# Token mixer of a diffusion trunk: the level scores as column-tiled products of 32 keys

## The chip, the cores and the metric

The kernel runs on one core of a Trainium2 chip. Its time is the device time of one execution in microseconds. Times are given as the median of several executions; a profiled execution is one more, recorded by the hardware profiler, and its trace tells which instruction ran when.

## The reference

The program is a two-layer backbone over 256 latent tokens and 256 context tokens of width 1024. Each layer is a half-step SwiGLU feed-forward, a token mixer and a second half-step feed-forward, each behind a modulated RMSNorm. The mixer has one input projection, two groups of heads and one output projection. The change is in the second group, a bidirectional gated linear recurrence with four heads of width 128:

```python
def step(S, inp):                       # one chunk of 64 tokens, one direction
    qc, kc, gc, vc = inp
    b = jnp.cumsum(gc, axis=2)
    diff = b[:, :, :, None, :] - b[:, :, None, :, :]
    decay = jnp.exp(jnp.where(mask, diff, -jnp.inf))
    scores = jnp.einsum("bhtk,bhsk,bhtsk->bhts", qc, kc, decay)
    o = (jnp.einsum("bhts,bhsv->bhtv", scores, vc)
         + jnp.einsum("bhtk,bhkv->bhtv", qc * jnp.exp(b), S))
    ...
```

In words: the score of query t against key s is a sum over the 128 channels of query, key and the product of all forget gates between the two tokens; the forward direction uses keys at or before t, the backward direction keys at or after t, and the outputs of both are added. The latent tokens start from the context's final state. In layer 1 only that state is needed of the context, not its output.

## The kernel before, in words

All activations lie with channels on the partitions. Every large product (feed-forwards, input and output projection) is a sum of three TensorE products in a split format: weights and activations are kept as a high part (`whi`, `h_hi`, `g_hi`) and the remainder (`wlo`, `h_lo`, `g_lo`), written by `mm3` at lines 309, 310 and 311. A weight piece of 512 x 256 comes in by one DMA into one of three `wraw` buffers; ScalarE makes its high part (`split`, line 210), VectorE its low part (`low`, line 214), into one of four slots of 4,352 bytes per partition each (`slot`). `pump` (lines 158 to 185) issues these steps as buffers come free.

The program is emitted in one fixed order. `fm` calls `tick` after each set of products, and `tick` advances one or two generators ("lanes") that stand behind the projection: their steps are placed among the large products after a set amount of these. So each engine gets its instructions in a written-out order, and a `yield n` in a generator says how much projection work comes before its next step.

The recurrence is the generator `hgrn`, one per layer and pair of heads. It replaces the chunked scan by seven levels over 128-token chunks. At level `lev`, with b = 2^lev, `lev` is the highest bit in which the positions of a valid pair differ, so the two tokens lie in the two halves of one block of 2b tokens. `KB` (keys) and `QA` (queries) have been multiplied by the forget gates up to the block's middle, so a plain product over channels is the score. `keys` (line 536, ScalarE) builds `ka`, in which each key carries the decay of the direction that its half needs; `alternate` reads the matching queries from both directions' `QA` with an access pattern that changes buffer every b elements.

`scores` (line 549) makes, for each head of the pair and each 128-token chunk, one fp32 product of 128 keys by 128 queries: 8 products in layer 0 (four chunks), 4 in layer 1 (two chunks), per call. There are eight calls per pair: one for the diagonal (`ks`, copied into the score tile `ST` by ScalarE at line 559), one per level. TensorE carries out an fp32 product as two instructions, each with a weight load. A 128 x 128 result holds all pairs of a chunk, of which each level needs only some: VectorE's `copy_predicated` (line 581) puts those into `ST` under a byte mask, `masks`, 128 x 128 per level. Between the products and the `copy_predicated`, VectorE multiplies `KB` (line 569), `QA` (line 575) and the gates `F` (line 578) for the next level. The score products go into PSUM tiles from a pool of three, `aux`, which the gated MLP heads (`spatial`, line 790) and the normalisations share. One score call takes two of them in layer 0, one in layer 1.

After the levels, scores between the two chunks of a sequence go into the middle slots of `ST` (lines 587 to 591), and `ST` multiplies the values (line 629).

One other place in the kernel uses products with 32 columns of weights: `ada_rows` (line 281), which sums the modulation's partial results. It writes four products to the four groups of 32 PSUM partitions:

```python
for n, (lhs, rhs) in enumerate(parts):
    for c in range(4):
        nc.tensor.matmul(ps[32 * c:32 * c + 32, :], lhsT=lhs, rhs=rhs[:, P * c:P * c + P],
                         start=(n == 0), stop=(n == len(parts) - 1))
```

Of the kernel before, what the change touches and what calls it, by code (L numbers as in the profile page):

```python
# [12 lines left out]
U8 = mybir.dt.uint8  # L13
AF = mybir.ActivationFunctionType
# [3 lines left out]
P = 128  # L18
# [11 lines left out]
EPS = 1e-6  # L30
POS_THETA = 10000.0
NLEV = 7
LEAD = 64
GLEAD = 0

# [16 lines left out]


def level_masks():
    x = np.arange(P)[:, None] ^ np.arange(P)[None, :]
    m = np.stack([(x >> lev) == 1 for lev in range(NLEV)], axis=1)
    return np.ascontiguousarray(m.reshape(P, NLEV * P).astype(np.uint8))

# [14 lines left out]
class Trunk:  # L75
# [129 lines left out]
    def slot(self, part, lead):  # L205
        t = self.wp.tile([P, LEAD + 1024], F32R, tag=part, name="w" + part, bufs=self.N_SPLIT)
        return t[:, lead:lead + 1024].rearrange("p (k c) -> p k c", k=4)
# [99 lines left out]
    def mm3(self, ps, l_hi, l_lo, r_hi, r_lo, start, stop, swap=False):  # L307
        mm = self.nc.tensor.matmul
        mm(ps, lhsT=l_hi, rhs=r_hi, start=start, stop=False)  # L309
        mm(ps, lhsT=l_hi, rhs=r_lo, start=False, stop=False)  # L310
        mm(ps, lhsT=l_lo, rhs=r_hi, start=False, stop=stop)  # L311
# [207 lines left out]
    def hgrn(self, l, hp, mp, F, KB, q, V, ready, oT, ended):  # L519
        nc = self.nc  # L520
        last = l == DEPTH - 1
        nq = SEQ if last else T
        ns = nq // SEQ
        nb = nq // P
# [3 lines left out]
        QA = mp.tile([P, 2, 2, nq], F32, tag="QA", name="QA", bufs=two)  # L528
        ST = mp.tile([P, 2, ns, 4, P], F32, tag="ST", name="ST", bufs=two)
        tt = nc.vector.tensor_tensor  # L530

        def keys(lev):
            b = 1 << lev
            ka = mp.tile([P, 2, nq], F32, tag="ks", name="ka", bufs=2 * two)
            for d in range(2):
                nc.scalar.activation(self.halves(ka, b)[d], self.halves(KB[:, d, :, :nq], b)[d], AF.Copy)
            return ka

        def scores(lhs, rhs):

            r = []
            for h in range(2):
                if h == 0 or ns == 2:
                    sc = self.aux()
                    dst = ST[:, h, :, 0::3, :] if ns == 2 else ST[:, :, 0, 0::3, :]
                    r.append((dst, sc.rearrange("p (s c t) -> p s c t", c=2, t=P)))
                for c in range(nb):
                    o = (c + (0 if ns == 2 else nb * h)) * P
                    nc.tensor.matmul(sc[:, o:o + P], lhsT=lhs(h, c * P), rhs=rhs(h, c * P), start=True, stop=True)  # L549
            return r  # L550

        ks = mp.tile([P, 2, nq], F32, tag="ks", name="ks", bufs=2 * two)
        tt(ks, KB[:, 0, :, :nq], KB[:, 1, :, :nq], op=ALU.add)
        ka = keys(0)
        for d in range(2):
            tt(QA[:, 1 - d], q[:, :, :nq], F[:, d, :, :nq], op=mult)
        yield HP[l]
        for dst, sc in scores(lambda h, c: ks[:, h, c:c + P], lambda h, c: q[:, h, c:c + P]):
            nc.scalar.activation(dst, sc, AF.Copy)
        yield HQ[l]  # L560
        for lev in range(NLEV):
            b = 1 << lev
            sc = scores(lambda h, c: ka[:, h, c:c + P],
                        lambda h, c: self.alternate(QA[:, 0, h, c:c + P], QA[:, 1, h, c:c + P], b))
            n = T // b
            for d in range(2):
                t = F[:, d, :, :n].rearrange("p h (n two) -> p h n two", two=2)
                kh = self.halves(KB[:, d], b)[d]
                tt(kh, kh, t[:, :, :, 1 - d, None].to_broadcast([P, 2, n // 2, b]), op=mult)
            if lev < NLEV - 1:  # L570
                ka = keys(lev + 1)
            for d in range(2):
                tq = F[:, d, :, :nq // b].rearrange("p h (n two) -> p h n two", two=2)
                qh = self.halves(QA[:, 1 - d], b)[1 - d]
                tt(qh, qh, tq[:, :, :, d, None].to_broadcast([P, 2, nq // (2 * b), b]), op=mult)
            for d in range(2):
                t = F[:, d, :, :n].rearrange("p h (n two) -> p h n two", two=2)
                tt(F[:, d, :, :n // 2], t[:, :, :, 0], t[:, :, :, 1], op=mult)
            mk = self.masks[:, lev, None, None, :].to_broadcast([P, 2, 2, P])
            for dst, s_ in sc:  # L580
                nc.vector.copy_predicated(dst, mk, s_)
            yield pace
        for h in range(2):
            sc = self.aux()
            for s in range(ns):
                c0, c1 = slice(s * SEQ, s * SEQ + P), slice(s * SEQ + P, s * SEQ + SEQ)
                nc.tensor.matmul(sc[:, s * SEQ:s * SEQ + P], lhsT=KB[:, 0, h, c0], rhs=QA[:, 1, h, c1],
                                 start=True, stop=True)
                nc.tensor.matmul(sc[:, s * SEQ + P:s * SEQ + SEQ], lhsT=KB[:, 1, h, c1], rhs=QA[:, 0, h, c0],
                                 start=True, stop=True)  # L590
            nc.scalar.activation(ST[:, h, :, 1:3, :], sc[:, :nq].rearrange("p (s c t) -> p s c t", c=2, t=P), AF.Copy)
        for d in range(2):
            for h in range(2):
                a = P * (1 - d)
                x = QA[:, 1 - d, h, a:a + P]
                nc.vector.tensor_scalar(x, x, F[:, d, h, d:d + 1], None, op0=mult)
                a = SEQ + P * d
                x = KB[:, d, h, a:a + P]
# [15 lines left out]
        for h in range(2):  # L614
            head = slice((2 * hp + h) * P, (2 * hp + h + 1) * P)
            for d in range(2):
                o = ps[:, (2 * h + d) * P:(2 * h + d + 1) * P]
# [4 lines left out]
        for s in range(ns):  # L622
            ps = self.adp.tile([P, 512], F32, tag="ada", name="o")
            for c in range(2):
                for h in range(2):
                    head = slice((2 * hp + h) * P, (2 * hp + h + 1) * P)
                    o = ps[:, (2 * c + h) * P:(2 * c + h + 1) * P]
                    for e in range(2):
                        nc.tensor.matmul(o, lhsT=ST[:, h, s, 2 * e + c, :], rhs=V[:, 2 * s + e, head],  # L629
                                         start=(e == 0), stop=(e == 1 and s == 1))  # L630
                    if s == 0:
                        for d in range(2):
                            nc.tensor.matmul(o, lhsT=QA[:, 1 - d, h, c * P:(c + 1) * P], rhs=S[:, h, d, :],  # L633
                                             start=False, stop=(d == 1))
# [5 lines left out]
            r = self.rstd(ss[:, :4], 4, P)  # L640
# [227 lines left out]
    def start(self):  # L868
        nc = self.nc
        io = self.io  # L870
        cp = self.cp
# [16 lines left out]
        self.mods = cp.tile([P, DEPTH * N_MOD, 2, KT], F32, tag="mods", name="mods")  # L888
        self.lb = cp.tile([P, 2, 2, 4], F32, tag="lb", name="lb")
        self.vec = [cp.tile([P, P], F32, tag=f"vec{l}", name="vec") for l in range(DEPTH)]  # L890
        self.masks = cp.tile([P, NLEV, P], U8, tag="masks", name="masks")
        with self.tc.tile_pool(name="start", bufs=1) as st:
            self.table(AF.Silu)
            cc = st.tile([16, P], F32, tag="cc", name="cc")
# [4 lines left out]
            for l, names in enumerate((("norm_ffn1_g", "norm_mix_g", "norm_ffn2_g", "norm_final_g"),  # L899
# [4 lines left out]
                for nm in names:  # L904
                    r = io[nm]
                    if nm != "norm_final_g":
                        r = r.rearrange("l n -> (l n)")
                    r = r.rearrange("(k p) -> k p", p=P)
# [91 lines left out]
            r = self.token_rstd(LAT)  # L1000
# [105 lines left out]
```

## Time and profile before

| | |
|---|---|
| median of 3 executions | 1790.61 us (1787.4 to 1796.05) |
| profiled execution | 1787.99 us, its span 1786.2 us |
| layer 0 mixer, recurrence's levels | about 450 to 598 us of the span |
| layer 1 mixer, recurrence's levels | about 1449 to 1537 us |
| score products, TensorE busy | 44.7 us (levels) and 6.1 us (diagonal) |
| `copy_predicated`, VectorE busy | 29.2 us |

In the profile, PE is TensorE's products, PEld its weight loads, DVE VectorE, ACT ScalarE, SP the engine that issues the DMAs. A line such as `L549 PE MATMUL aux<-QA,ka 128*128 128x128 f32 x336 | 44.7, 285 | 0.0` reads: source line, engine, operation, output and inputs, weights (rows*columns), moving operand, number of instructions, then busy time in us, mean duration in ns, and idle time before. In a timeline, the first number is the start in us, the second the length of the merged run of instructions. Products overlap in TensorE's pipeline, so the distance between starts, not the duration, is the rate.

### The profile page before, as it was taken

What the parts mean: (1) busy time and instruction counts of PE and PEld (TensorE: products, weight loads), DVE (VectorE), ACT (ScalarE), POOL (GpSimd) and SP (SyncE); (2) the same over time, 40 slices, a digit from 0 to 9 for tenths busy, and PEclk for the clock granted to TensorE, in tenths of its full rate; (3) what the DMA queues carried; (4) which work ended last, traced back from release to release, by engine and by line L of the source; (5) the groups of instructions that cost most, each with busy time, mean ns of one, the idle gap of its engine ahead of it and who ended that gap; (6) DMA issues with size and microseconds to landing.
All of it is one profiled execution on the core that took longest, in us unless ns stands there. A gap on an engine that the chain in (4) does not pass through costs nothing. (4 is left out here: it accounts for less than half of the span.)

```text
span 1786.2 us, 27050 instructions
## 1 busy us (share of the span) xinstructions
PE 1753.0 (98%) x10853; PEld 1534.5 (86%) x10853; DVE 1129.6 (63%) x1746; ACT 670.5 (38%) x1087; POOL 19.6 (1%) x26
## 2 busy tenths in 40 slices
PE   6999999999999999999999999999999999989998
PEld 5788888899899898888888898888888999979998
DVE  4876676775737667666666676555545668665554
ACT  3422222236545344222222252223222565545543
POOL 0000000000000000000000000000000000000000
PEclk9999999999999999999999999999999999989999
DMA  8565655664212114555555545555454532446663
GB/s 315 166 177 162 178 160 165 180 188 139 71 60 83 60 60 144 151 157 160 151 153 158 178 137 157 161 154 159 156 167 153 160 107 83 130 125 195 194 186 128
DMA packets 230646, 266.65 MB, mean 149 GB/s; under 512 B 10369, under 2 KB 192377, under 8 KB 230521
## 3 DMA queue, kind: packets, MB, share of 16 engines
q1 hardware_dynamic: 230520, 264.93, 48.8%
q8 instruction: 85, 1.39, 0.3%
q14 instruction: 41, 0.33, 0.1%
HBM read 263.84 MB, written 1.05 MB: 148 GB/s over the span
## 5 line engine op out<-in xcount | busy, mean ns | idle before, releaser
L309 PE MATMUL mm<-h_hi,whi 128*128 128x512 f32 (+1 forms) x2016 | 704.2, 349 | 4.7 <-ACT h_hi L406 3.0
L310 PE MATMUL mm<-h_lo,whi 128*128 128x512 f32 (+1 forms) x2016 | 696.8, 346 | 1.7 <-DVE h_lo L395 1.4
L311 PE MATMUL mm<-h_hi,wlo 128*128 128x512 f32 (+1 forms) x2016 | 694.1, 344 | 0.0
L214 DVE TENSOR_TENSOR wlo<-wraw,whi 128x1024 fp32r<-128x1024 f32 x362 | 430.8, 1196 | 320.0 <-ACT whi L210 318.9
L210 ACT ACTIVATE whi<-wraw 128x1024 fp32r<-128x1024 f32 x362 | 370.9, 1032 | 393.3 <-PE mm L310 271.5
L309 PEld LDWEIGHTS mm<-h_hi,whi 128*128 128x128 f32 x2016 | 380.5, 189 | 56.3 <-ACT h_hi L406 4.0
L310 PEld LDWEIGHTS mm<-h_lo,whi 128*128 128x128 f32 x2016 | 380.8, 189 | 50.7 <-DVE h_lo L395 6.0
L311 PEld LDWEIGHTS mm<-h_hi,wlo 128*128 128x128 f32 x2016 | 380.7, 189 | 47.2
L272 DVE SCALAR_TENSOR_TENSOR acc<-wada,cond,acc 128x512 f32<-128x512 f32 x392 | 275.7, 748 | 35.5 <-DMA wada<-in_w_ada_dram 33.9
L309 PE MATMUL mm<-g_hi,whi 128*128 128x256 f32 (+1 forms) x836 | 279.9, 335 | 0.0
L311 PE MATMUL mm<-g_hi,wlo 128*128 128x256 f32 (+1 forms) x836 | 276.7, 331 | 0.0
L310 PE MATMUL mm<-g_lo,whi 128*128 128x256 f32 (+1 forms) x836 | 276.7, 331 | 0.0
L309 PEld LDWEIGHTS mm<-g_hi,whi 128*128 128x128 f32 x836 | 157.3, 188 | 18.3 <-issue 2.4
L311 PEld LDWEIGHTS mm<-g_hi,wlo 128*128 128x128 f32 x836 | 157.2, 188 | 15.8
L310 PEld LDWEIGHTS mm<-g_lo,whi 128*128 128x128 f32 x836 | 157.1, 188 | 15.2
L210 ACT ACTIVATE g_hi<-silu 128x512 fp32r<-128x512 f32 (+1 forms) x92 | 51.7, 562 | 179.2 <-DVE silu L449 179.2
L447 ACT ACTIVATE silu<-mm 128x512 f32<-128x512 f32 (+1 forms) x92 | 48.2, 527 | 134.3 <-PE mm L311 134.3
L214 DVE TENSOR_TENSOR g_lo<-silu,g_hi 128x512 fp32r<-128x512 f32 (+1 forms) x92 | 55.7, 606 | 57.8 <-ACT g_hi L210 57.8
L449 DVE TENSOR_TENSOR silu<-silu,mm 128x512 f32<-128x512 f32 (+1 forms) x92 | 55.0, 598 | 28.6 <-PE mm L311 28.5
L309 PE MATMUL mm<-whi,h_hi 128*128 128x256 f32 x224 | 64.0, 286 | 0.0
L310 PE MATMUL mm<-wlo,h_hi 128*128 128x256 f32 x224 | 62.3, 278 | 0.0
L311 PE MATMUL mm<-whi,h_lo 128*128 128x256 f32 x224 | 62.2, 278 | 0.0
(128 smaller groups left out, 1055.1 us busy)
## 6 DMA issues: line engine op xcount, KB each, us to landing
wraw<-in_ffn_w_dram SPq DMA_DIRECT2D x271, 512.0 KB, 4.5
wada<-in_w_ada_dram SPq DMA_DIRECT2D x256, 256.0 KB, 3.0
wraw<-in_w_in_dram SPq DMA_DIRECT2D x56, 512.0 KB, 4.0
a<-in_w_ada_dram SPq DMA_DIRECT2D x8, 1024.0 KB, 9.8
wraw<-in_w_out_dram SPq DMA_DIRECT2D x16, 512.0 KB, 4.1
wraw<-in_ffn_w_dram SPq DMA_DIRECT2D x19, 256.0 KB, 2.7
x<-in_x_dram SPq DMA_DIRECT2D x2, 512.0 KB
ctx<-in_ctx_dram SPq DMA_DIRECT2D x2, 512.0 KB, 5.6
```

The costliest lines, as they stand in the source:

```text
L210: self.nc.scalar.activation(hi, src, AF.Copy)
L214: self.nc.vector.tensor_tensor(lo, src, hi.bitcast(F32), op=ALU.subtract)
L272: nc.vector.scalar_tensor_tensor(acc[:, s], raw, c, acc[:, s], op0=ALU.mult, op1=ALU.add)
L309: mm(ps, lhsT=l_hi, rhs=r_hi, start=start, stop=False)
L310: mm(ps, lhsT=l_hi, rhs=r_lo, start=False, stop=False)
L311: mm(ps, lhsT=l_lo, rhs=r_hi, start=False, stop=stop)
L447: nc.scalar.activation(silu[j], ps, AF.Silu)
L449: nc.vector.tensor_tensor(silu[j], silu[j], ps, op=ALU.mult)
```

## The change

- `scores` makes four products per head and chunk in place of one: 32 keys as weights by w queries, each to its own group of 32 PSUM partitions. For the diagonal and levels 0 to 4 the 32 queries are those of the same 32 tokens; at level 5 they are the neighbouring 32 tokens, at level 6 (w = 64) the other half's 64 tokens. All of a call now fits one `aux` tile: at most 128 x 512, in layer 0's level 6.
- For the diagonal and levels 0 to 4 the compact scores are collected in `cs`, the first 64 elements of a middle slot of `ST`: ScalarE copies the diagonal, VectorE's `copy_predicated` puts in each level under a mask of 32 x 32 per block (`masks` shrinks to five levels). Level 5 and 6 need no mask: `place` (ScalarE) copies them block by block from PSUM into `ST`. At level 5, `place` also copies `cs` to the diagonal blocks of `ST`, four copies of 32 partitions.
- The mask tile takes 384 bytes per partition in place of 896, 512 less, so tiles allocated after it move by 512 bytes. The order of the work, the `yield`s and everything else are as they were.

```diff
 def level_masks():
-    x = np.arange(P)[:, None] ^ np.arange(P)[None, :]
-    m = np.stack([(x >> lev) == 1 for lev in range(NLEV)], axis=1)
-    return np.ascontiguousarray(m.reshape(P, NLEV * P).astype(np.uint8))
+    x = (np.arange(P) % Q)[:, None] ^ np.arange(Q)[None, :]
+    m = np.stack([(x >> lev) == 1 for lev in range(NLOW)], axis=1)
+    return np.ascontiguousarray(m.reshape(P, NLOW * Q).astype(np.uint8))
...
-        def scores(lhs, rhs):
-
-            r = []
+        def scores(lhs, rhs, w=Q):
+
+            sc = self.aux()[:, :2 * nb * w]
             for h in range(2):
-                if h == 0 or ns == 2:
-                    sc = self.aux()
-                    dst = ST[:, h, :, 0::3, :] if ns == 2 else ST[:, :, 0, 0::3, :]
-                    r.append((dst, sc.rearrange("p (s c t) -> p s c t", c=2, t=P)))
                 for c in range(nb):
-                    o = (c + (0 if ns == 2 else nb * h)) * P
-                    nc.tensor.matmul(sc[:, o:o + P], lhsT=lhs(h, c * P), rhs=rhs(h, c * P), start=True, stop=True)
-            return r
-
+                    o = (nb * h + c) * w
+                    for e in range(4):
+                        nc.tensor.matmul(sc[Q * e:Q * e + Q, o:o + w], lhsT=lhs(h, c * P + Q * e), rhs=rhs(h, c * P, e),
+                                         start=True, stop=True)
+            return sc.rearrange("p (n c t) -> p n c t", c=2, t=w)
+
+        def place(sc, p0, p1, t0, w):
+            nc.scalar.activation(ST.rearrange("p h s e t -> p (h s) e t")[p0:p1, :, 0::3, t0:t0 + w], sc[p0:p1], AF.Copy)
+
+
+        cs = ST.rearrange("p h s e t -> p (h s) e t")[:, :, 1, :2 * Q].rearrange("p n (c t) -> p n c t", t=Q)
...
-        for dst, sc in scores(lambda h, c: ks[:, h, c:c + P], lambda h, c: q[:, h, c:c + P]):
-            nc.scalar.activation(dst, sc, AF.Copy)
+        sc = scores(lambda h, o: ks[:, h, o:o + Q], lambda h, o, e: q[:, h, o + Q * e:o + Q * e + Q])
+        nc.scalar.activation(cs, sc, AF.Copy)
...
-            sc = scores(lambda h, c: ka[:, h, c:c + P],
-                        lambda h, c: self.alternate(QA[:, 0, h, c:c + P], QA[:, 1, h, c:c + P], b))
+            keyed = lambda h, o: ka[:, h, o:o + Q]
+            if lev < NLOW:
+                sc = scores(keyed, lambda h, o, e: self.alternate(*(QA[:, d, h, o + Q * e:o + Q * e + Q]
+                                                                    for d in range(2)), b))
+            else:
+
+                u = lambda e: 1 - (Q * e // b) % 2
+                m = lambda e: Q * e // (2 * b) * 2 * b + u(e) * b
+                sc = scores(keyed, lambda h, o, e: QA[:, u(e), h, o + m(e):o + m(e) + b], b)
...
-            mk = self.masks[:, lev, None, None, :].to_broadcast([P, 2, 2, P])
-            for dst, s_ in sc:
-                nc.vector.copy_predicated(dst, mk, s_)
+            if lev < NLOW:
+                mk = self.masks[:, lev, None, None, :].to_broadcast([P, ns * 2, 2, Q])
+                nc.vector.copy_predicated(cs, mk, sc)
+            else:
+                for p0 in range(0, P, b):
+                    place(sc, p0, p0 + b, p0 ^ b, b)
+            if lev == NLOW:
+                for p0 in range(0, P, Q):
+                    place(cs, p0, p0 + Q, p0, Q)
...
-        self.masks = cp.tile([P, NLEV, P], U8, tag="masks", name="masks")
+        self.masks = cp.tile([P, 384], U8, tag="masks", name="masks")[:, :NLOW * Q].rearrange("p (l t) -> p l t", t=Q)
```

`Q` is 32, `NLOW` is 5, `NLEV` is 7, `P` is 128; `nb` is the number of chunks (4 in layer 0, 2 in layer 1), `ns` that of sequences (2 and 1).

More of the change, by code (lines that the diff above doesn't have):

```diff
@@ L32 @@
 NLEV = 7
+Q = 32
+NLOW = 5
 LEAD = 64
```

## The prediction

> **What bounds the kernel now.** I read the page first, then the groups by form, then TensorE's timeline at the score products.
>
> ```profile
> span 1786.2 us, 27050 instructions
> PE 1753.0 (98%) x10853; PEld 1534.5 (86%) x10853; DVE 1129.6 (63%) x1746; ACT 670.5 (38%) x1087; POOL 19.6 (1%) x26
> PE   6999999999999999999999999999999999989998
> PE 40%; DVE 2%; ACT 1%; issue 0%; DMA 0%; POOL 0%; ACTq 0%; DVEq 0%; POOLq 0%
> ```
>
> TensorE (PE) is at 98% and its digits stand at 9 through both mixers. The chain that ended last runs over PE almost alone (40% of the span against 3% for VectorE and ScalarE). So a change is worth what it takes from TensorE's stream of instructions; time taken from VectorE counts only where TensorE waits for it.
>
> ```profile
> L549 PE MATMUL aux<-QA,ka 128*128 128x128 f32 x336 | 44.7, 285 | 0.0
> L549 PEld LDWEIGHTS aux<-QA,ka 128*128 128x128 f32 x336 | 43.2, 192 | 1.2
> L549 PE MATMUL aux<-q,ks 128*128 128x128 f32 x48 | 6.1, 276 | 0.2 <-DVE ks L553 0.2
> L281 PE MATMUL ada_ps<-acc,sel 128*32 128x128 f32 x448 | 19.1, 280 | 0.9 <-DVE acc L272 0.7
> L281 PEld LDWEIGHTS ada_ps<-acc,sel 128*32 128x32 f32 x448 | 10.3, 109 | 12.1 <-issue 11.1 <-PE mm L311 0.5 <-DVE acc L272 0.4
> ```
>
> The score products are 336 + 48 = 384 instructions (192 products, two instructions each) with next to no wait. L281 is the same form as the new products, 32 columns of weights into four groups of PSUM partitions, but with 128 moving columns. It is the nearest row for the new cost. The timeline of PE shows what a block of score products costs between ordinary products:
>
> ```profile
> 469.64 0.39 PE L311 MATMUL mm<-h_hi,wlo 128*128 128x512 f32 x1
> 469.87 1.95 PE L549 MATMUL aux<-QA,ka 128*128 128x128 f32 x16
> 471.57 0.48 PE L309 MATMUL mm<-h_hi,whi 128*128 128x512 f32 x1
> 471.89 0.40 PE L310 MATMUL mm<-h_lo,whi 128*128 128x512 f32 x1
> ...
> 455.04 2.82 PE L549 MATMUL aux<-QA,ka 128*128 128x128 f32 x16
> ...
> 463.16 2.09 PE L549 MATMUL aux<-QA,ka 128*128 128x128 f32 x16
> ...
> 1449.56 0.39 PE L311 MATMUL mm<-h_hi,wlo 128*128 128x512 f32 x1
> 1449.79 1.05 PE L549 MATMUL aux<-q,ks 128*128 128x128 f32 x8
> 1450.60 0.48 PE L309 MATMUL mm<-h_hi,whi 128*128 128x512 f32 x1
> 1450.91 0.40 PE L310 MATMUL mm<-h_lo,whi 128*128 128x512 f32 x1
> ```
>
> From the start of the product before to the start of the second product after are 2.25 us in layer 0; two ordinary spacings (0.23 each, 469.64 to 469.87) taken off, 1.80 us are the block's. In layer 1: 1.35 - 0.45 = 0.90. That is about 0.11 us per instruction. Level 0 (2.82, its queries read one element from each buffer in turn) is 0.87 longer than 1.95, so 2.67; level 1 (2.09) is 0.14 longer, 1.94. One pair of heads costs 6 x 1.80 + 2.67 + 1.94 = 15.4 us in layer 0 and half, 7.7, in layer 1.
>
> **The change, part by part.** *The products.* Each instruction becomes four (1,536 in place of 384), of 32 weights' columns and 32 moving columns (64 at level 6). What four such instructions, a quartet, cost:
>
> ```profile
> 1093.10 0.39 PE L311 MATMUL mm<-h_hi,wlo 128*128 128x512 f32 x1
> 1093.41 0.65 PE L281 MATMUL ada_ps<-acc,sel 128*32 128x128 f32 x16
> 1093.99 0.50 PE L309 MATMUL mm<-h_hi,whi 128*128 128x512 f32 x1
> 1094.33 0.40 PE L310 MATMUL mm<-h_lo,whi 128*128 128x512 f32 x1
> ...
> 1160.38 0.39 PE L311 MATMUL mm<-h_hi,wlo 128*128 128x512 f32 x1
> 1160.69 0.43 PE L281 MATMUL ada_ps<-acc,sel 128*32 128x128 f32 x8
> 1161.05 0.50 PE L309 MATMUL mm<-h_hi,whi 128*128 128x512 f32 x1
> 1161.39 0.39 PE L310 MATMUL mm<-h_lo,whi 128*128 128x512 f32 x1
> ```
>
> The same subtraction gives 1.23 - 0.45 = 0.78 us for 16 and 1.01 - 0.45 = 0.56 for 8. So two quartets cost 0.22, one 0.11, and what is left, 0.56 - 0.22 = 0.34 us, is a toll that the block pays for going to the narrow form and back (the gap ahead, 0.31 in place of 0.23, and the slow pair behind). Narrowing the answer to TensorE's first 0.1 us of that block, and the durations of L281:
>
> ```profile
> 1093.41 0.32 PE L281 MATMUL ada_ps<-acc,sel 128*32 128x128 f32 x4
> ...
> L281 PE MATMUL ada_ps<-acc,sel x448: 269/273/297, 75.4 to 1384.1; 128*32 128x128 f32 x150
> ```
>
> Four products of 297 ns (the longest, those behind an empty pipeline) all lie within 320: they start about 7 ns apart, so the four column groups do run at once. A quartet with 128 columns takes as long as one full product, 0.11, so it is the streaming of its columns that sets it, as far as this shows. With 32 columns that falls to 0.11 / 4 = 28 ns, and four starts 7 ns apart are 28 as well. A load of 32 columns takes 297 - 273 = 24 ns. If load and product overlap, a quartet costs 28 ns; one after the other, 24 + 28 = 52. I take 40, the middle, since the trace has no such short product, and keep 28 and 52; the far end is 0.11, no shrinking at all.
>
> Layer 0's block of 16 quartets then costs 16 x 0.040 + 0.34 = 0.98 (diagonal and levels 2 to 5); level 0, slowed like its wide form by 2.67 / 1.80 = 1.5, 0.96 + 0.34 = 1.30; level 1 by 1.08, 1.03; level 6 has 32 more columns, 28 ns a quartet, 1.43. Sum 5 x 0.98 + 1.30 + 1.03 + 1.43 = 8.7 against 15.4. Layer 1 (8 quartets): 5 x 0.66 + 0.82 + 0.68 + 0.88 = 5.7 against 7.7. With two pairs each: 2 x 6.7 + 2 x 2.0 = 17.4.
>
> ```profile
> 1486.89 2.38 PE L549 MATMUL aux<-QA,ka 128*128 128x128 f32 x16
> 1494.57 2.01 PE L549 MATMUL aux<-QA,ka 128*128 128x128 f32 x16
> ...
> 597.81 1.06 PE L790 MATMUL aux<-wsT,vt 128*128 128x128 f32 x8
> 600.29 0.91 PE L790 MATMUL aux<-wsT,vt 128*128 128x128 f32 x6 [1.42 <-DVE ST L581]
> ```
>
> Twice in layer 1 the blocks of both pairs stand back to back (x16) and pay the toll once: 0.7 less. *The PSUM tiles.* The L790 product waits 1.42 us for `copy_predicated` to free one of the three `aux` tiles, since the last score call holds two. It will hold one, so the wait goes: 1.4. What is late next there is the weighting of the gated MLP on VectorE, whose queue gets shorter too. Sum: 17.4 + 0.7 + 1.4 = 19.5 us.
>
> *VectorE and ScalarE.*
>
> ```profile
> L581 DVE COPY_PREDICATED ST<-masks,aux 128x512 f32<-128x512 uint8 x42 | 29.2, 731 | 0.0
> L559 ACT ACTIVATE ST<-aux 128x512 f32<-128x512 f32 x6 | 3.6, 596 | 7.3 <-PE aux L549 7.3
> L210 ACT ACTIVATE whi<-wraw 128x1024 fp32r<-128x1024 f32 x343 | 358.9, 1054 | 342.0 <-PE mm L310 253.4 <-issue 72.7 <-DMA wraw<-in_ffn_w_dram 8.7
> 450.00:500.00 50.00, 49.75 (x309) 44.82 (x309) 36.76 (x60) 23.36 (x36) 0.00 (x0) 1.00 0.24 75
> 1480.00:1530.00 50.00, 50.00 (x437) 50.00 (x436) 37.90 (x79) 26.13 (x69) 2.64 (x2) 1.00 0.28 85
> ```
>
> VectorE loses 42 masked copies of 512 elements and gets 20 of 256 or 128, at 0.2 to 0.73 us each: 15 to 25 us less, all beside PE (no wait of PE in the levels but those named), so worth nothing. ScalarE gets, per pair, eight copies of 32 partitions at level 5 and two of 64 at level 6, at most 0.6 us each like L559: up to 6 us, in layer 0 about 3 at once. They wait for products and a `copy_predicated` of a level earlier, long done. Behind them in ScalarE's queue stand the weight splits and the evacuations of projection tiles. ScalarE is busy 23 and 26 of 50 us there, and its splits mostly wait for PE to free a slot (253 of 342 us idle), so four slots' worth of work ahead covers 3 us; without that cover the price is 3 us a pair, 12 in all.
>
> *Addresses.* Weight tiles move by 512 bytes against the activations. The four weight slots lie 4,352 bytes apart, so every other one by an odd multiple of 512, and they run alike; I cost this at nothing, up to 2.6% of the 180 us of the last feed-forward (20 us hold 177 products of 256 columns there, against 138 in 16 us elsewhere), 4.7 us:
>
> ```profile
> 1620.00:1640.00 20.00, 16.24 (x59) 11.02 (x60) 1.00 0.66 192
> 382.00:398.00 16.00, 12.68 (x46) 8.43 (x45) 1.00 0.67 215
> ```
>
> (both of line 310 alone, one of three alike.)
>
> The profiled execution took 1787.99 us: it would take 1768.5 (span 1766.7). The median of the three runs, 1790.61, lies 2.6 above it; 1790.6 - 19.5 gives the forecast, 1771.
>
> **The rivals.** *Starts are rationed.* Each quartet is eight instructions, loads included. The trace shows 7 ns between starts for four in a row only; over a long run L281's quartets come every 0.11 us, 14 ns an instruction. If instructions come more slowly than the products run, at 65 ns a quartet say, 25 ns x 384 = 9.6 us of the gain are lost: 1781 (52 to 85 ns give 1776 to 1788).
>
> *A floor under every product.* L281's products start 27 ns apart on average (0.22 us for eight). If that is no effect of their 128 columns but a floor for any product, a quartet stays at 0.11 us: 70 ns x 384 = 27 us more than at 40, 1798. Against it speak the 7 ns between single starts. The Trainium skill states such a floor ("TensorE: Matmul & The Clock Gate", section "Wait — 56ns, not 53.3ns?"): start to start never under about 25 ns, however few the columns; an estimate by it is 100 ns a quartet and 1794. The trace agrees with that at most for products in the same columns.
>
> *The load sets the pace (slower).* A load's row says 109 ns. If a column group's next load starts only behind the start of its product, and the next product waits for all of the load, a quartet takes 109 + 7 = 116 ns at any width: 76 ns x 384 = 29 us more than at 40, 1800. It decides from 91 ns a quartet on, where the tolls (30 blocks x 0.34 = 10 us) eat the gain. For it: L281's 0.11 fits a load as well as a stream. Against: full loads last 192 ns by their row and yet follow at 0.11, so a load's duration isn't its spacing, and the 24 ns above.
>
> *The addresses matter after all*: 1771 + 4.7 = 1775.7.
>
> **How the numbers follow.** Forecast 0.63, rationed starts 0.14, floor 0.08, load 0.10, addresses 0.05. A measurement of this kernel tells about 0.5% (9 us) from no change. Forecast, addresses and half of the rationed case are faster by more: 0.75. The other half and the floor (7 us over the median before) lie within: 0.15. The load case is slower: 0.10. The forecast alone holds 28 to 52 ns, 1766.4 to 1775.6, and some 3 us of tolls and of runs on either side: 1763 to 1779. The range takes in the rationed case, 1763 to 1788, and leaves out floor and load, 0.18.
>
> **What would show it.** L549 has 1,536 products of 128*32; a layer 0 block of 64 lasts about 0.6 us between its first start and the next L309, and the L309 to L310 step behind it is about 0.34. The 1.42 us wait of L790 is gone, `copy_predicated` is x20, and ordinary products keep 0.23 and 0.113. I am wrong if a quartet takes 0.1 us or more, if the toll per block is well over 0.34, or if PE gets waits for ScalarE behind level 5.

## The result, and the profile after

The changed kernel takes 1764.83 us (median of 3 executions, 1763.34 to 1765.01), against 1790.61 before: a ratio of 0.985, with a 95% interval of 0.982 to 0.988. The profiled execution of the changed kernel also took 1764.83 us, 23.2 less than the profiled one of before. The prediction was 1771, a gain of 19.5.

The head of the page of the changed kernel, and the shares of its chain that ended last:

```profile
span 1763.1 us, 29359 instructions
PE 1732.1 (98%) x12005; PEld 1504.9 (85%) x12005; DVE 1108.3 (63%) x1724; ACT 681.8 (39%) x1125; POOL 19.7 (1%) x26
PE 38%; DVE 2%; ACT 2%; issue 0%; DMA 0%; POOL 0%; ACTq 0%; DVEq 0%; POOLq 0%
```

TensorE has 1,152 more instructions than before (12,005 products against 10,853) and is busy for 20.9 us less. It still bounds the kernel at 98%. VectorE lost 21 us, ScalarE gained 11. Since the diff moves lines, the three split products are now L311 to L313, the scores L548, `place` L553, `copy_predicated` L593 and the gated MLP's product L808.

The groups by form of the changed kernel (instructions, then busy us and mean ns, then idle time before):

```profile
L548 PE MATMUL aux<-QA,ka 128*32 128x32 f32 x1152 | 15.3, 201 | 0.0
L548 PE MATMUL aux<-QA,ka 128*32 128x64 f32 x192 | 3.5, 221 | 0.0
L548 PE MATMUL aux<-q,ks 128*32 128x32 f32 x192 | 2.4, 198 | 0.4 <-DVE ks L558 0.4
L593 DVE COPY_PREDICATED ST<-masks,aux 128x256 f32<-128x256 uint8 x10 | 4.4, 441 | 0.0
L593 DVE COPY_PREDICATED ST<-masks,aux 128x128 f32<-128x128 uint8 x10 | 3.0, 297 | 0.0
L553 ACT ACTIVATE ST<-ST 32x256 f32<-32x256 f32 x8 | 3.3, 415 | 0.1
L553 ACT ACTIVATE ST<-aux 64x512 f32<-64x512 f32 x4 | 2.4, 591 | 0.0
```

All 1,536 products of 32 weight columns are there. Their busy time is 15.3 + 3.5 + 2.4 = 21.2 us, where it was 50.8. The masked copies cost VectorE 7.4 us instead of 29.2. The `place` copies (six forms, two of them shown) add 14.8 us to ScalarE.

TensorE's timeline of the changed kernel at a layer 0 block, a layer 1 block, a level 0 block and a level 6 block, in that order (start in us, length, instructions merged into the row):

```profile
467.13 0.39 PE L313 MATMUL mm<-h_hi,wlo 128*128 128x512 f32 x1
467.45 0.76 PE L548 MATMUL aux<-QA,ka 128*32 128x32 f32 x64
468.14 0.50 PE L311 MATMUL mm<-h_hi,whi 128*128 128x512 f32 x1
468.48 0.40 PE L312 MATMUL mm<-h_lo,whi 128*128 128x512 f32 x1
...
1448.36 0.39 PE L313 MATMUL mm<-h_hi,wlo 128*128 128x512 f32 x1
1448.68 0.46 PE L548 MATMUL aux<-QA,ka 128*32 128x32 f32 x32
1449.07 0.50 PE L311 MATMUL mm<-h_hi,whi 128*128 128x512 f32 x1
1449.40 0.39 PE L312 MATMUL mm<-h_lo,whi 128*128 128x512 f32 x1
...
548.52 0.39 PE L313 MATMUL mm<-h_hi,wlo 128*128 128x512 f32 x1
548.84 0.89 PE L548 MATMUL aux<-QA,ka 128*32 128x32 f32 x64
549.66 0.50 PE L311 MATMUL mm<-h_hi,whi 128*128 128x512 f32 x1
550.00 0.39 PE L312 MATMUL mm<-h_lo,whi 128*128 128x512 f32 x1
...
582.79 1.10 PE L548 MATMUL aux<-QA,ka 128*32 128x64 f32 x64
583.83 0.94 PE L808 MATMUL aux<-wsT,vt 128*128 128x128 f32 x6
```

By the prediction's subtraction (start of the product before to start of the second product after, less 0.45) the layer 0 block costs 468.48 - 467.13 - 0.45 = 0.90 us, where it was 1.80. The layer 1 block costs 1449.40 - 1448.36 - 0.45 = 0.59, where it was 0.90. The level 0 block, that of the second pair of heads, costs 1.03 (2.67 before); that of the first pair, at 455 us, costs 1.30, of which 0.24 us is a gap between two of its products that no wait in the trace explains. The difference of the first two, 0.31 us for eight quartets, gives 39 ns for a quartet, and what is left of the layer 1 block, 0.59 - 8 x 0.039 = 0.28, is the toll. At level 6 the L808 product follows the scores without a wait: the 1.42 us of before are gone.

Where the 23.2 us lie: added up by the starts of their products, the 30 blocks cost 46.5 us before and 25.6 after, 21.0 less; the wait of L808 gives 1.4; some 0.8 is spread over the rest of the span. Laid beside each other, the ordinary products of the two traces show where the gap opens: the change is 0.9 us behind ahead of layer 0's levels and 15.5 us ahead at their end, and gains another 5.5 us in layer 1's levels. Over all that lies between and behind the levels the gap moves by less than 2 us.

### The profile page after: what moved, and what is told of

Its sections match the earlier page's. It is cut to its first block, busy times and chain, and to the rows that moved or that the text cites. A ratio compares the mean times of both kernels' runs of the same rounds, so it can differ in the third digit from the quotient of the medians.

```text
span 1763.1 us, 29359 instructions
## 1 busy us (share of the span) xinstructions
PE 1732.1 (98%) x12005; PEld 1504.9 (85%) x12005; DVE 1108.3 (63%) x1724; ACT 681.8 (39%) x1125; POOL 19.7 (1%) x26
## 5 line engine op out<-in xcount | busy, mean ns | idle before, releaser
L311 PE MATMUL mm<-h_hi,whi 128*128 128x512 f32 (+1 forms) x2016 | 703.6, 349 | 5.0 <-ACT h_hi L408 3.0
L313 PE MATMUL mm<-h_hi,wlo 128*128 128x512 f32 (+1 forms) x2016 | 693.4, 344 | 0.0
L311 PEld LDWEIGHTS mm<-h_hi,whi 128*128 128x128 f32 x2016 | 380.0, 188 | 57.8 <-issue 4.0
L313 PEld LDWEIGHTS mm<-h_hi,wlo 128*128 128x128 f32 x2016 | 380.1, 189 | 47.1
L311 PE MATMUL mm<-g_hi,whi 128*128 128x256 f32 (+1 forms) x836 | 279.8, 335 | 0.0
L313 PE MATMUL mm<-g_hi,wlo 128*128 128x256 f32 (+1 forms) x836 | 276.6, 331 | 0.0
L311 PEld LDWEIGHTS mm<-g_hi,whi 128*128 128x128 f32 x836 | 157.3, 188 | 18.3 <-issue 2.4
L313 PEld LDWEIGHTS mm<-g_hi,wlo 128*128 128x128 f32 x836 | 157.1, 188 | 15.9
L451 DVE TENSOR_TENSOR silu<-silu,mm 128x512 f32<-128x512 f32 (+1 forms) x92 | 55.0, 598 | 29.2 <-PE mm L313 29.0
L311 PE MATMUL mm<-whi,h_hi 128*128 128x256 f32 x224 | 64.3, 287 | 0.0
L313 PE MATMUL mm<-whi,h_lo 128*128 128x256 f32 x224 | 62.5, 279 | 0.0
```

The lines of the kernel that those rows point to most:

```text
L451: nc.vector.tensor_tensor(silu[j], silu[j], ps, op=ALU.mult)
```

## The experiments

Theory: TensorE's stream is the bound. A quartet in four column groups costs about 40 ns, with a toll of about 0.3 us for each block; VectorE and ScalarE are covered; a shift of 512 bytes costs nothing. The rivals tested here are that the gain is VectorE's relief, that it comes with the narrow weights in any order, that load and product run one after the other, and that the addresses decide. The kernel before was measured again on the same chip with each group of experiments: medians 1789.56, 1789.80 and 1790.09 us. All ratios are against it.

**The order of the column groups.** All products of one column group stand behind each other, instead of the four groups in turn:

```diff
-            for h in range(2):
-                for c in range(nb):
-                    o = (nb * h + c) * w
-                    for e in range(4):
+            for e in range(4):
+                for h in range(2):
+                    for c in range(nb):
+                        o = (nb * h + c) * w
```

> The changed kernel with the same products in another order: all of a call's products for one group of 32 columns, then all for the next group, so that neighbours in the stream use the same columns. Results, counts and widths are the same. Theory (four column groups run at once, and a quartet lasts 33 ns because of it): products in the same columns must follow one another at about 30 ns instead of 8, so a layer 0 block of 64 grows from 0.90 to 64 x 0.030 + 0.34 = 2.3 us and a layer 1 block of 32 from 0.59 to 1.3; 16 x 1.4 + 16 x 0.7 = 33 us, some 1797 us, ratio to before 1.00 to 1.01. If load and product do not overlap inside one group, 50 ns each and some 1830. Rival (the narrow width alone makes the gain, wherever the products stand): no change from 1765.

Measured: 1795.7 us, 1.0036 of before (1.0011 to 1.006). TensorE's timeline of this kernel, at a layer 0 block:

```profile
471.82 0.39 PE L313 MATMUL mm<-h_hi,wlo 128*128 128x512 f32 x1
472.14 1.91 PE L548 MATMUL aux<-QA,ka 128*32 128x32 f32 x64
473.98 0.50 PE L311 MATMUL mm<-h_hi,whi 128*128 128x512 f32 x1
474.32 0.39 PE L312 MATMUL mm<-h_lo,whi 128*128 128x512 f32 x1
```

The same 64 products now cost 474.32 - 471.82 - 0.45 = 2.05 us, more than the 1.80 of the wide ones. Within a column group their starts are mostly 32 ns apart in the trace; in the change the starts follow at 6 to 7 ns within a quartet and at about 12 ns between quartets. Four starts then take some 32 ns, so each column group starts about as often as here, and four of them do so at once. The 32 ns also speak against load and product one after the other, for which the expectation gave 50: they overlap within a single column group too. So the whole gain hangs on four neighbours going to four different column groups; the change in this other order is slower than the kernel before. The Trainium skill ("TensorE: Matmul & The Clock Gate", section "Wait — 56ns, not 53.3ns?") names about 25 ns as the least distance from start to start. The 32 ns within one column group agree with it; the changed kernel's own row does not:

```profile
L548 PE MATMUL aux<-QA,ka x64: 196/196/218, 467.4 to 468.0; 128*32 128x32 f32 x64
```

This is the view of that one block (durations in ns as least, median and longest, then the first and the last start). 64 products of at most 218 ns fit into 0.76 us, so the 63 steps take about 0.56 us, 9 ns each. Between its four column groups this kernel shows no such floor.

**The narrow weights without the narrow answers.** The kernel before, with each 128 x 128 score product as four products of 32 weight columns by all 128 queries:

```diff
-                    nc.tensor.matmul(sc[:, o:o + P], lhsT=lhs(h, c * P), rhs=rhs(h, c * P), start=True, stop=True)
+                    for e in range(4):
+                        nc.tensor.matmul(sc[32 * e:32 * e + 32, o:o + P], lhsT=lhs(h, c * P)[:, 32 * e:32 * e + 32],
+                                         rhs=rhs(h, c * P), start=True, stop=True)
```

> The kernel before with one part of the change alone: each 128 x 128 score product is made as four products of 32 columns of weights by 128 moving columns, side by side; evacuation, masks and VectorE's work as before. Theory (the quartet's time is the streaming of its moving columns, and going to the narrow form and back costs a toll of 0.34 us a block): a quartet stays at 0.11 us and only the toll comes on top, 30 x 0.32 = 9 to 10 us, 1800, ratio 1.005. Rival (it is the column groups as such that are fast): a time between 1765 and 1785.

Measured: 1797.73 us, 1.0058 (1.0037 to 1.0079). TensorE's timeline at the layer 0 block:

```profile
470.49 0.39 PE L311 MATMUL mm<-h_hi,wlo 128*128 128x512 f32 x1
470.81 1.95 PE L550 MATMUL aux<-QA,ka 128*32 128x128 f32 x64
472.69 0.50 PE L309 MATMUL mm<-h_hi,whi 128*128 128x512 f32 x1
473.03 0.39 PE L310 MATMUL mm<-h_lo,whi 128*128 128x512 f32 x1
```

The block costs 473.03 - 470.49 - 0.45 = 2.09 us against 1.80: quartets of 128 columns take the 0.11 us of one wide product, and 0.29 us of toll comes on top. Over the 30 blocks that is 55.8 us against 46.5, as the total shows within its interval. So narrow weights alone save nothing: the saving is the 96 columns that are no longer streamed, and the toll is the price of the form. The Trainium skill ("TensorEngine Tiling (Array Packing)", section "Key Properties") says that changing the tiling mode drains the array, without a figure. Both traces have longer steps at the two places: the step into the block is 0.32 us instead of 0.23, and the first step behind it 0.34. That a drain makes them longer fits, but no run here shows it by itself.

**VectorE's relief given back.** Each `copy_predicated` of levels 0 to 4 runs four times (the repeats write the same values):

```diff
-                nc.vector.copy_predicated(cs, mk, sc)
+                for _ in range(4):
+                    nc.vector.copy_predicated(cs, mk, sc)
```

> The changed kernel with every masked copy of levels 0 to 4 issued four times (the repeats write the same values), which brings VectorE's work in the levels back to about that of before (20 copies become 80, some 30 us in place of 7.4). Theory (VectorE lies beside TensorE): 1765 to 1767, ratio to before 0.986. Rival (part of the gain is VectorE's relief): 5 to 15 us of the gain are lost, 1770 to 1780.

Measured: 1769.93 us, 0.9892 (0.9875 to 0.9908), 5.1 above the change. The groups of this kernel, and the one wait of TensorE over a microsecond that its timeline has in the levels:

```profile
L594 DVE COPY_PREDICATED ST<-masks,aux 128x256 f32<-128x256 uint8 x40 | 17.8, 446 | 1.0
L594 DVE COPY_PREDICATED ST<-masks,aux 128x128 f32<-128x128 uint8 x40 | 12.1, 302 | 1.0
```

```profile
579.13 0.75 PE L548 MATMUL aux<-QA,ka 128*32 128x32 f32 x64 [1.30 <-DVE ST L594]
```

VectorE carries 29.9 us of masked copies again, slightly more than before, and the time rises by a fifth of the total gain, not by all of it. The theory missed by 3 to 5 us here; the time stands at the lower edge of what the rival gave. The wait shows the way: the scores of a level need an `aux` tile in PSUM that a longer copy holds. Laid beside the change, product by product, the trace loses 2.1 us in the levels, 1.8 in layer 0 and 0.3 in layer 1. Another 1.3 us is lost ahead of the first split product and 0.9 in the stretch of 30 us ahead of layer 1's levels, where the edit adds nothing. So the trace shows VectorE's shorter copies to be worth about 2 us, by freeing PSUM tiles earlier; the rest of the gain is TensorE's.

**ScalarE's cover.** Each copy of `place` runs twice, 15 us more for ScalarE:

```diff
-            nc.scalar.activation(ST.rearrange(...)[p0:p1, :, 0::3, t0:t0 + w], sc[p0:p1], AF.Copy)
+            for _ in range(2):
+                nc.scalar.activation(ST.rearrange(...)[p0:p1, :, 0::3, t0:t0 + w], sc[p0:p1], AF.Copy)
```

> The changed kernel with each of ScalarE's block copies of levels 5 and 6 issued twice (the repeats write the same values): ScalarE gets 15 us more in four places. Theory (ScalarE's copies are covered by the weight splits that lie ahead): 1765 to 1766, ratio 0.986. Rival (the copies hold up splits or evacuations, so the change pays for them already): 3 to 10 us more, 1768 to 1775.

Measured: 1780.57 us (1773.84 to 1785.62), 0.9942 (0.992 to 0.9964). The theory fails, and the time is beyond the rival's too: 15 us of work on an engine that is busy for 39% cost 15.7 us at the median, with executions 12 us apart. Two rows of TensorE's timeline of this kernel:

```profile
1488.49 0.46 PE L548 MATMUL aux<-QA,ka 128*32 128x32 f32 x32 [1.94 <-ACT ST L610]
...
1532.66 0.71 PE L809 MATMUL aux<-wsT,vt 128*128 128x128 f32 x4 [1.45 <-ACT ST L610]
```

And two stretches of 10 us, of this kernel (length, then busy time and instructions of PE, PEld, DVE, ACT and POOL, then the granted clock, DMA share and GB/s):

```profile
1480.00:1490.00 10.00, 8.06 (x93) 7.86 (x94) 8.85 (x24) 5.50 (x13) 0.00 (x0) 0.94 0.36 109
1490.00:1500.00 10.00, 10.00 (x108) 9.83 (x108) 7.10 (x16) 6.16 (x15) 0.00 (x0) 0.89 0.23 58
```

and of the changed kernel:

```profile
1480.00:1490.00 10.00, 10.00 (x143) 9.66 (x142) 8.85 (x24) 6.36 (x14) 0.00 (x0) 1.00 0.14 38
1490.00:1500.00 10.00, 10.00 (x90) 10.00 (x89) 4.10 (x9) 6.38 (x23) 0.00 (x0) 1.00 0.41 125
```

L610 is ScalarE's copy of the scores between the two chunks out of an `aux` tile, and it stands behind the copies of `place`. When it comes late, TensorE waits for the tile. Right behind the wait of 1.94 us the granted clock is half for 3.4 us, so the wait costs more than its length:

```profile
1488.85:1492.26 3.41, 3.41 (x27) 3.39 (x17) 3.41 (x13) 1.10 (x3) 0.00 (x0) 0.50 0.02 5
```

The two profiled executions are 14.3 us apart. Laid beside each other, product by product, they part by 7.0 us between layer 1's first score product and the L809 product above, where the copies of `place` came to 6.1 us more. In layer 0's levels and right behind them it is 1.7 us, for 8.7 us more of copies. About 3 us lie behind layer 1's mixer, most of it in another stretch at a clock of 0.50 (1560.53 to 1567.36), and some 2.5 us in places that have no such copies. So layer 0's copies are largely covered and layer 1's are not; how much of the rest is the copies' doing is not shown. Layer 1's levels take 81 us against 132 in layer 0, for the same number of copies. In the change itself only one wait for L610's copy (L609 there) is left, 0.23 us at L808.

**The addresses.** The change pads the mask tile (160 bytes of masks) to 384, which keeps all addresses behind it the same modulo 512. First without padding:

```diff
-        self.masks = cp.tile([P, 384], U8, tag="masks", name="masks")[:, :NLOW * Q].rearrange("p (l t) -> p l t", t=Q)
+        self.masks = cp.tile([P, NLOW * Q], U8, tag="masks", name="masks")[:, :NLOW * Q].rearrange("p (l t) -> p l t", t=Q)
```

> The changed kernel with a mask tile of just the 160 bytes per partition that it needs in place of 384: tiles allocated after it lie 224 bytes lower than in the changed kernel, which is no multiple of 512. Theory (the ordinary products' spacing depends on where weights and activations lie to each other, as the 113 and 116 ns in different stretches of the trace before suggest, so the padding to 384 is worth something): 1768 to 1785, with 512-column products off 227 ns or 256-column products off 113 in places. Rival (addresses do nothing): 1765, all spacings as they were.

Then with 896 bytes in place of 384, so that nothing moves against the kernel before:

> The changed kernel with the mask tile of the old size, 896 bytes per partition: no tile after it moves against the kernel before. Theory (a shift of 512 bytes is worth nothing): 1765, within 2 us of the changed kernel. Rival (the shift itself brought part of the gain or took some): 3 us or more to either side.

Measured: 1794.67 us without padding, 1.0026 (1.0014 to 1.0038): the whole gain is lost. With 896 bytes 1764.74, 0.986 (0.9843 to 0.9876): the same as the change. So a shift by 512 is indeed worth nothing, and a shift by 224 more costs 30 us. It is in no wait and in no block of scores, but in the ordinary products that read `h`. The stretch of the first feed-forward, the `h_lo` product alone (one of three alike; PE busy, PEld busy, granted clock, DMA share, GB/s), of the changed kernel:

```profile
60.00:300.00 240.00, 133.03 (x342) 64.06 (x341) 1.00 0.57 169
```

without padding:

```profile
60.00:300.00 240.00, 131.58 (x333) 62.66 (x334) 1.00 0.56 164
```

and with 896 bytes:

```profile
60.00:300.00 240.00, 132.99 (x342) 64.04 (x341) 1.00 0.58 169
```

The same stretch at the same granted clock holds 333 products instead of 342, 2.6% fewer. From start to start, products of 512 columns that stream `h` go from 227.5 to 233.3 ns on average, those of 256 columns from 115.4 to 119.1. Products that stream `g`, whose tiles are allocated behind the mask tile like the weights and move with them, keep 227 and 115 to 116. With 3 x 1,184 and 3 x 832 products of `h`, that is 3,552 x 5.8 + 2,496 x 3.7 = 30 us, the whole loss.

Three more paddings ask which distance counts. Each is the same line with another size, 352, 320 or 256 bytes, a shift of 32, 64 or 128 bytes against the change:

> The changed kernel with a mask tile of 352 bytes: tiles behind it lie 32 bytes lower. The run with 160 bytes (224 lower) cost 1.6% in ordinary products. Theory A (a shift matters modulo 64 bytes, and 224 is 32 over a multiple of 64): this one costs as much, some 1790. Theory B (modulo 512: only the size of the shift within 512 counts): somewhere between 1765 and 1795. Theory C (multiples of 32 bytes are harmless, something else in the 160-byte run was at fault): 1765.

> The changed kernel with a mask tile of 320 bytes: tiles behind it lie 64 bytes lower. Theory A (modulo 64): no cost, 1765. Theory B (modulo 512): a cost, some 1775 to 1795. Theory C: 1765.

> The changed kernel with a mask tile of 256 bytes: tiles behind it lie 128 bytes lower. Theory A (modulo 64): no cost, 1765. Theory B (modulo 512): a cost, some 1775 to 1795; if the period is 128, no cost here but one with 64 bytes.

Measured: 1794.26 us (1.0022, 1.0006 to 1.0039) at 32 bytes, 1781.23 (0.9958, 0.9945 to 0.9972) at 64, 1792.01 (1.0007, 0.9992 to 1.0022) at 128. Multiples of 64 cost too, so the residue modulo 64 does not decide; each of the four shifts within 512 bytes that were tried has a cost of its own, 16 to 30 us. The same view as above, for 352, 320 and 256 bytes:

```profile
60.00:300.00 240.00, 131.68 (x334) 62.61 (x333) 1.00 0.56 163
```

```profile
60.00:300.00 240.00, 133.00 (x340) 63.75 (x339) 1.00 0.57 167
```

```profile
60.00:300.00 240.00, 131.87 (x335) 62.97 (x334) 1.00 0.57 165
```

Again only products of `h` are slower: 233.3, 229.0 and 232.5 ns on average at 512 columns (in the order of the fences). At 64 bytes the long products are nearly spared, but those of 256 columns are the slowest of all, 121 ns, which no count in this stretch shows. Why the distance counts stays open: everything behind the mask tile moved together, the raw weight pieces and temporaries too, and no run moved the weights alone. The kernel, before and after, also sets each weight piece at 0, 128 or 192 bytes from the start of its slot, by which product reads it (`lead`); no run tried another residue with other leads.

**Saving a toll.** Since each block pays the toll, the diagonal's products were put next to level 0's, so that two calls share one:

```diff
-        yield HP[l]
+        yield HP[l] + HQ[l]
...
-        yield HQ[l]
```

> The changed kernel with the diagonal's score products moved down to stand right ahead of level 0's, so that four of the 30 blocks join others; the work is the same. Theory (each block pays a toll of about 0.3 us for going to the narrow form and back): 4 x 0.3 = 1.2 us less, 1763.5, seen in the trace as four blocks of 128 or 64 products with one entry and one exit. Rival (the toll is the block's own drain and scales with its products, or level 0 now waits for a PSUM tile): no gain, or a wait ahead of level 0.

Measured: 1768.62 us (1763.84 to 1771.21), 0.9879 (0.986 to 0.9899): no gain that can be seen. TensorE's timeline of this kernel at a joint block:

```profile
548.38 0.39 PE L313 MATMUL mm<-h_hi,wlo 128*128 128x512 f32 x1
548.70 0.76 PE L548 MATMUL aux<-q,ks 128*32 128x32 f32 x64
549.31 0.89 PE L548 MATMUL aux<-QA,ka 128*32 128x32 f32 x64
550.13 0.50 PE L311 MATMUL mm<-h_hi,whi 128*128 128x512 f32 x1
550.47 0.40 PE L312 MATMUL mm<-h_lo,whi 128*128 128x512 f32 x1
```

The joint block costs 550.47 - 548.38 - 0.45 = 1.64 us, against 0.90 + 1.03 apart: 0.29 less, one toll. That would be just over 1 us for four pairs; but in layer 1's second pair the products now come earlier than their operands (a wait of 0.21 us ahead of the joint block and a gap of 0.31 us inside it), and the four executions differ by 7 us, far more than the saving. The toll is shown, its saving in the total is not.

## Why the prediction was right, and where its steps were off

**The bound** was right. The gain is in TensorE's stream and stays through everything behind it; putting VectorE's work back (29.9 us) takes 5 of the 25 us away, 2 of them in the levels. Of the 6.2 us between the forecast and the measured median, 3.7 come from the sum (23.2 against 19.5); the other 2.6 are the distance between median and profiled execution before, which the changed kernel does not have.

**The quartet** came out right, with some luck: 38 to 39 ns where 40 was taken, as the middle between 28 (load and product overlap) and 52 (they do not). The overlap is what the runs show. In the trace the first eight quartets of a layer 0 block come every 32 ns, the two in the middle take 43 and 48, and the later ones come every 33 to 34: near the 28, and far from the 65 ns of the rival with rationed starts. Why the middle is slower is not shown.

**The sizes around it** were set too high, by the steps "what is left, 0.56 - 0.22 = 0.34 us, is a toll" and "level 0, slowed like its wide form by 2.67 / 1.80 = 1.5". The toll is 0.28 (0.29 in the second experiment). A quartet of level 0 takes 44 ns in the trace, where the prediction's 0.96 us for sixteen means 60, and without the unexplained gap of the first pair the block costs 1.03 to 1.06, not 1.30. Level 6 costs 1.23 in layer 0, not 1.43. So the blocks gave 21.0 us where 17.4 + 0.7 were summed, which is most of the 3.7. A slow-down measured on a wide product (reading every element from another buffer) did not carry over in proportion to the short one.

**The PSUM tile** was right, 1.4 us, and nothing came late in its place beyond 0.23 us. The third experiment adds that VectorE "worth nothing" was a little short: shorter copies free the same tiles.

**ScalarE's cover** was right in its outcome and wrong in its reason. The prediction's "four slots' worth of work ahead covers 3 us" looked at the splits of weights. What TensorE waits for first is the tile behind L610, and the fourth experiment shows that in layer 1 a further 6.1 us of copies cost 7.0. The change came out without that price, but in layer 1 it had little cover to spare. A low share of busy time was no sign of slack there.

**The addresses** were right for the shift that the change makes, and wrong in the price: "up to 2.6% of the 180 us of the last feed-forward" took one stretch as all that could be hit, for 4.7 us. Measured, another residue reaches the products of `h` throughout and costs 16 to 30 us, as much as the change gains. The line on the mask tile, which looks like housekeeping, decides whether there is a gain to speak of.

**The rivals** fall: a floor under every product by the 9 ns between starts, the load that sets the pace by the 39 ns quartet. Their times, 1798 and 1800, would have been close with the products in another order: 1795.7 us in the first experiment.

## What to carry to other kernels

Here the small products gained from 32-column weights only because neighbours in the stream go to different column groups, only by the columns they no longer stream, and only as far as that saving exceeds a toll of 0.3 us for going in and out of each block. Before timing a change that resizes any tile, hold the addresses of all other tiles to their residues (here modulo 512 bytes), or the change may be measured together with another spacing of the large products. Test the slack of a covered engine by doubling its new work, not by its share of busy time.

## What the runs showed of the hardware that was not expected

- Split products of 512 columns run at 227 or up to 233 ns, those of 256 columns at 115 to 121 ns, when nothing but the size of one small tile is changed, and with it the distance in memory between the weights and `h`, at a granted clock of 1.00 in the stretches compared. Shifts of 32, 64, 128 and 224 bytes cost 29, 16, 27 and 30 us of 1765; 512 bytes cost nothing.
- Narrow fp32 products (32 weight columns, 32 moving columns) in four column groups in turn start 9 ns apart over 64 in a row, in one column group 32 ns apart.
- Right behind one wait of TensorE of 1.94 us, the granted clock was 0.50 for 3.4 us (0.94 and 0.89 over the two stretches of 10 us around it).
